# A hybrid decoder step on one core: state loads moved within the scans, and one activation table loaded ahead

## The chip, the cores and the metric

The kernel runs on one core of a Trainium2 chip. The metric is device time in microseconds (us), the median of several runs; less is better. The core's engines are called by these names in the profile: PE is TensorE (matmuls; PEld is its weight load), DVE is VectorE, ACT is ScalarE, POOL is GpSimd, SP is SyncE. Each works through a queue of its own in order. Here SyncE and GpSimd also issue nearly all the DMAs; "POOLq" and "SPq" are the issuing sides of these engines.

## The reference

One layer of a hybrid decoder for a prompt of 256 tokens and for 8 samples of 4 tokens each, which share the weights. Cut to what matters here:

```python
xn = _rmsnorm(x, norm_mix)
z, xbc, dt_raw, q, k, v, r, g_lr, gate_a, gate_b = _split(xn @ w_in, IN_SIZES)
xbc = silu(causal_dwconv(xbc));  xs, Bm, Cm = _split(xbc, ...)
dt = softplus(dt_raw + ssd_dt_bias);  A = -exp(ssd_A_log)
y_ssd, ssd_state_new = _ssd_scan(xs_h, dt, A, Bm, Cm, ssd_state)       # 4 groups of 8 heads
u = (y_ssd + ssd_D * xs_h) * silu(z)
u = u * rsqrt(mean(u * u, axis=-1) + EPS) * ssd_norm                   # per group
branch_a = u @ w_ssd_out
glog = log_sigmoid(g_lr @ w_gla_gate + b_gla_gate) / GATE_TAU
o, gla_state_new = _gla_scan(qh, kh, vh, glog, gla_state)              # 4 heads
o = o * rsqrt(mean(o * o, axis=-1) + EPS) * gla_norm * silu(r)
branch_b = o @ w_gla_out
h = x + (sigmoid(gate_a) * branch_a + sigmoid(gate_b) * branch_b) @ w_mix_out
h = h + cross_attend(_rmsnorm(h, norm_cross), mem_k, mem_v, w_cq, w_co)
up = causal_dwconv(_rmsnorm(h, norm_ffn) @ w_up);  a, gt = split(up)
h = h + (silu(gt) * a) @ w_down
```

All states (`state_ssd`, 8 samples x 32 heads x 64 x 128, and others) are read and their new values written.

## The kernel before

All activations are held transposed, channels on partitions and the 288 tokens (256 of the prompt, 32 of the samples) along the free axis. A projection (`proj`, lines 133 to 169) runs over blocks of 256 output columns and, inside, over the 16 blocks of input channels, two at a time: `wload` (108) has SyncE load 256 KB of weights into one of six `raw` buffers; `wsplit` (100) lets ScalarE round them to `whi` (line 103) and VectorE subtract to `wlo` (105), five buffers of each; then 12 matmuls (148, 149, 153) of 288 columns use them up. When a block is done, ScalarE or VectorE copies its accumulators out of PSUM, for instance into `vT` (1044) or added into `ma` (1034).

The middle of the kernel (lines 1353 to 1364) goes through eight units n: four groups of the state-space branch (`ssd_scan`, line 743) and four heads of the gated linear attention (`gla_scan`, 1109). While the scan of unit n runs in the background, step by step (`weave`, 176), the main stream projects the inputs of unit n+1 (`ssd_proj`, `gla_proj`), then after 16 steps the output of unit n-1 (`project`), and in some units a few blocks of the gate (`gate_early`, 1295, with a Tanh on ScalarE for each block t and a store to `ga_d`). In n=2 and n=3 the first 20 background steps have TensorE's order written out by hand; everything else is put in order by a planner, which simulates the engines and issues what is ready, earlier lines first. DMAs marked `keep_in_program_order` stay in the order of the program.

A state-space scan first loads decays (`load_decay`, 749, tile `ab`, and `mab`, 759), transposes B, C and x, forms the decay matrices `m` (856, 859: Relu and Exp on ScalarE) in a loop over u = 0, 1, 2, whose products run one u later (870 to 892), and after that loop turns to the samples. Their states come twice: as `sin` by `load_state` (762; 2 DMAs of 256 KB for two samples, updated at 951 and stored at 956 by SyncE), and as `sqr` by `load_square` (772; 4 DMAs of 64 KB for one sample, transposed by VectorE into `st` at 941 for the products of line 927). `sin` and `m` share the six buffers of tag `c4`; `ab`, `sqr`, the gates and others share the seven of `e2`. GpSimd issues all these loads.

Each scan ends in `finish` (1005): the sum of squares by a matmul with ones (1013), `rstd_from` (230: logarithm at 232, exponential at 233), then the scaling into `un` (1021, 197, 198), which the output projection reads. `decays` (1058) of a GLA head uses Exp and Ln (1070, 1071) and later Exp (1077). Before the FFN `rstd_of` (1473) forms one more such norm. An activation function needs its table in ScalarE; where the set that is loaded lacks the function, the build puts an ACT_TABLE_LOAD in front, under the line of the function. Line 286 loads the set `LNEXP` ahead, for the norms of the first part.

Of the kernel before, what the change touches and what calls it, by code (L numbers as in the profile page):

```python
# [8 lines left out]
F32 = mybir.dt.float32  # L9
# [7 lines left out]
P = 128  # L17
# [25 lines left out]
def hybrid_step(ctx: ExitStack, tc: tile.TileContext, I: dict, O: list):  # L43
# [31 lines left out]
    ones = const.tile([P, P], F32, name="ones")  # L75
    V.memset(ones, 1.0)
    epsc = const.tile([P, 3], F32, name="epsc")
    V.memset(epsc[:, 0:1], EPS)
    V.memset(epsc[:, 1:2], 4.0 * EPS)
    fold4 = const.tile([P, NS], F32, name="fold4")  # L80
# [145 lines left out]

    def two(u, n):
        return lambda k: (u[:, k, :], u[:, n + k, :])

    def rstd_from(pl, ssq, n, four=False):  # L230
        r = pl.tile([P, T], F32, tag="rstd", bufs=1, name="rstd")
# [453 lines left out]
    def rep4(src, name):  # L685

        n = src.shape[1]
        o = b2(name).rearrange("p (t r s) -> p t r s", r=4, s=NS)[:, 0:n]
        V.tensor_copy(o, src.unsqueeze(2).to_broadcast([P, n, 4, NS]))
        return o.rearrange("p t r s -> p t (r s)")  # L690
# [52 lines left out]
    def ssd_scan(g, xsT, sz):  # L743
# [18 lines left out]
        def load_state(q):  # L762
            sin = c4([P, 2, 512], "sin")
            for e in range(2):
                tc.keep_in_program_order(G.dma_start(
                    out=sin[:, e, :].rearrange("p (t n) -> p t n", n=P),
                    in_=I["state_ssd"][2 * q + e, h0:h0 + 8].rearrange("(t e) x n -> (e x) t n", e=2)))
            sins.append(sin)
# [11 lines left out]


        bsr = rep4(bT[:, SEQ:T].unsqueeze(1), "bsr")
        yield
        a = mm_tile()
        MM(a[:, 0:256], bT[:, 0:P], cT[:, 0:SEQ], start=True, stop=True)
# [61 lines left out]
        for u in range(3):  # L847
            if u < 2:
                m = c4([P, 4, SEQ], "m")
                ea = b2("ea").rearrange("p (r n) -> p r n", n=P)  # L850
                for w in range(2):
                    ab, rr = abs_[2 * u + w], slice(2 * w, 2 * w + 2)
                    for r in range(2):
                        h = h0 + 4 * u + 2 * w + r
                        for c in range(2):
                            S.activation(m[:, 2 * w + r, c * P:(c + 1) * P], ab[:, r, c * P:(c + 1) * P], ACT.Relu,
                                         scale=-1.0, bias=tokc[:, c, 32 + h:33 + h])
                    S.activation(ea[:, rr], ab[:, :, P:SEQ], ACT.Exp)
                    S.activation(m[:, rr], m[:, rr], ACT.Exp, scale=-1.0)
                    if u == 0:  # L860
                        load_decay(2 + w)
                    yield
                    V.tensor_tensor(m[:, rr], m[:, rr],
                                    cbm.rearrange("p c n -> p (c n)").unsqueeze(1).to_broadcast([P, 2, SEQ]), ALU.mult)
                    V.tensor_tensor(ea[:, rr], ea[:, rr], cbx.unsqueeze(1).to_broadcast([P, 2, P]), ALU.mult)
                    yield
            if prev is not None:
                uu, pm, pea = prev
                a = mm_tile()
                for w in range(2):  # L870
                    o = w * SEQ
                    for s in range(3):
                        for e in range(2):
                            q = 2 * w + e
                            hs = slice((4 * uu + q) * 64, (4 * uu + q + 1) * 64)
                            rows = slice(64 * e, 64 * e + 64)
                            if s == 0:
                                MM(a[rows, o:o + P], xdt[0][:, hs], pm[:, q, 0:P], start=True, stop=True)
                            elif s == 1:
                                MM(a[rows, o + P:o + SEQ], xdt[1][:, hs], pm[:, q, P:SEQ], start=True, stop=False)  # L880
                            else:
                                MM(a[rows, o + P:o + SEQ], wx[0][:, hs], pea[:, q, :], start=False, stop=True)
                if u == 2:
                    axs = mm_tile()
                    for t in range(4):
                        TR(axs[:, t * P:(t + 1) * P], xsr[:, t, :], ident)
                for w in range(2):
                    tt = 2 * uu + w
                    tmp = th_tile()
                    V.scalar_tensor_tensor(tmp[:, 0:SEQ], xsT[:, tt, 0:SEQ], dcol[:, 4 * g + tt:4 * g + tt + 1],  # L890
                                           a[:, w * SEQ:(w + 1) * SEQ], ALU.mult, ALU.add)
                    V.tensor_tensor(sz[:, tt, 0:SEQ], tmp[:, 0:SEQ], sz[:, tt, 0:SEQ], ALU.mult)
            if u < 2:
                prev = (u, m, ea)
            if u == 1:
                xsr = rep4(xsT[:, :, SEQ:T], "xsr")
            yield
        for b in range(NSQ):
            load_square(b)
        load_state(0)  # L900
        load_state(1)

        diag(cdm, cT[:, SEQ:T])
        for r in range(2):
            S.activation(mss[:, r, :], mab[:, r, :], ACT.Relu, scale=-1.0, bias=acs[:, 2 * g + r:2 * g + r + 1])
# [27 lines left out]
        for hf_ in range(2):  # L933
            bblk = r2("bblk").rearrange("p (b n) -> p b n", n=P)
            V.tensor_tensor(bblk, bst.unsqueeze(1).to_broadcast([P, 4, P]),
                            bmask[:, 4 * hf_:4 * hf_ + 4].unsqueeze(2).to_broadcast([P, 4, P]), ALU.mult)
            pair = sins[2 * hf_:2 * hf_ + 2]

            def turned(b):
                st = b2("st")  # L940
                V.transpose(st, sqs[b])
                if b + NSQ < NB:
                    load_square(b + NSQ)
                sts.append(st)

            def updated(t):
                a = mm_tile()
                MM(a, wst[:, t * P:(t + 1) * P], bblk.rearrange("p b n -> p (b n)"), start=True, stop=True)  # L948
                for b in range(4):
                    sl_ = pair[b // 2][:, b % 2, t * P:(t + 1) * P]  # L950
                    V.scalar_tensor_tensor(sl_, sl_, elcol[:, 4 * g + t, 4 * hf_ + b:4 * hf_ + b + 1],
                                           a[:, b * P:(b + 1) * P], ALU.mult, ALU.add)
                if t % 2:
                    for b in range(4):
                        hh = h0 + 2 * (t - 1)
                        nc.sync.dma_start(
                            out=o_sssd[4 * hf_ + b, hh:hh + 4].rearrange("(t e) x n -> (e x) t n", e=2),
                            in_=pair[b // 2][:, b % 2, (t - 1) * P:(t + 1) * P].rearrange("p (t n) -> p t n", n=P))

            for x in range(4):  # L960
                turned(4 * hf_ + x)
                yield 1.5
                if x % 2 == 0:
                    continue
                for t in ((0, 1) if x == 1 else (2, 3)):
                    updated(t)
                    if hf_ == 0 and t < 2:
                        load_state(2 + t)
                    yield 1.5
        inter()  # L970
        yield
# [33 lines left out]
    def finish(u, sq, gcol, four):  # L1005

        if len(fin) < 7:
            sp = b2r("sqh")[:, 0:T], b2r("sql")[:, 0:T]
            split(*sp, sq)
            yield  # L1010
            ssq = mm_tile()
            for w in range(2):
                MM(ssq[:, 0:T], ones.bitcast(F32R), sp[w], start=(w == 0), stop=(w == 1))
        else:
            ssq = mm_tile()
            MM(ssq[:, 0:T], ones, sq, start=True, stop=True)
        rstd = rstd_from(pa, ssq[:, 0:T], 512, four)
        yield
        un = pa.tile([P, 8, T], F32R, tag="un", bufs=1, name="un")
        for t in range(4):  # L1020
            V.tensor_tensor(u[:, t, :], u[:, t, :], rstd, ALU.mult)
            split_from(un[:, t, :], un[:, 4 + t, :], u[:, t, :], gcol[:, t:t + 1])
            if t % 2:
                yield
        fin.append(un)
# [14 lines left out]
    def gla_proj(h, out):  # L1040
# [17 lines left out]
        def decays():  # L1058
# [8 lines left out]
                S.activation(qe[:, k, :], a[:, 0:T], ACT.Identity, bias=vec("b_gla_gate")[:, 2 * h + k:2 * h + k + 1])  # L1067
            yield
            S.activation(ke, qe, ACT.Abs)
            S.activation(ke, ke, ACT.Exp, scale=-1.0)  # L1070
            S.activation(ke, ke, ACT.Ln, bias=1.0)
            V.scalar_tensor_tensor(qe, qe, 0.0, ke, ALU.min, ALU.subtract)
# [217 lines left out]
            yield from proj(I["w_in"], o + 256 * j2, 256, X, KT, cons)  # L1290

    gq = []
    GH = KT // 4

    def gate_early(t, a):

        if t % 2 == 0:
            gq.append(e2("gq"))
        S.activation(gq[-1][:, t % 2, :], a, ACT.Tanh, scale=0.5)
        if t % 2:  # L1300
            G.dma_start(out=ga_d[:, t - 1:t + 1, :], in_=gq[-1])

# [169 lines left out]

    def rstd_of():
        ssq = mm_tile()
        tc.keep_in_program_order(MM(ssq[:, 0:T], ones, rst.pop(), start=True, stop=True))
        return rstd_from(pb, ssq[:, 0:T], D)

    rst = []
# [508 lines left out]
```

## Time and profile before

| | us |
|---|---|
| median of 3 runs | 2479.48 (2479.35 to 2480.06) |
| the profiled execution | 2484.3 |
| its span | 2482.6 |
| TensorE busy in it | 2466.2 |
| ScalarE busy in it | 1355.8 |

The span is what the trace covers, from the first to the last instruction; the execution's own time is 1.7 us longer. The profiled execution is 4.8 us above the median of the runs without a profile. A matmul's end is modelled, so busy time of PE counts matmuls that overlap only once. In a row by line stand the line, the engine, the operation, its tiles (out<-in), how often, then busy us and mean ns, then the idle time before. In a row of waits stand who waited, for whom, the total, the times and the longest. In a row by stretch stand the stretch, the sum, each engine's busy time with its number of instructions, the granted clock of PE (1.00 is full), the mean busy share of the 16 DMA engines, and GB/s.

### The profile page before, as it was taken

The page shows a single profiled execution, that of the slowest core. Times are in us where ns is not written, and L with a number is a line of the kernel's source. Part 1 is how long each engine was busy: PE and PEld are TensorE (multiplying, and loading weights), DVE is VectorE, ACT ScalarE, POOL GpSimd, SP SyncE. Part 2 cuts the span into 40 slices and gives each one's busy share as a digit, 9 for nine tenths or more (in the row PEclk, how much of TensorE's full clock was granted, in tenths as well). Part 3 has the DMA queues.
Part 4 walks back from the last instruction along what each step waited for, and adds up shares of the span by engine and source line. Part 5 has one row for each costly group of instructions (what it writes and reads, how often), then busy time and mean ns, then how long its engine had stood idle before and what let it go on. Part 6 is the DMA issues. An engine that isn't in the chain of part 4 may idle for free.

```text
span 2482.6 us, 52113 instructions
## 1 busy us (share of the span) xinstructions
PE 2466.2 (99%) x18738; PEld 2388.1 (96%) x18738; DVE 1775.2 (72%) x3804; ACT 1355.8 (55%) x2781; POOL 439.2 (18%) x798
## 2 busy tenths in 40 slices
PE   9999999999999999999999999999999999999998
PEld 8889999999999999999999989999999999999998
DVE  6866778896777766777666577667777676676766
ACT  6766647646464655554455545455555454554545
POOL 3102144143111010110111122402111001020012
PEclk9999999999999999999999999999999999999999
DMA  8877697787768686777778599655555555555555
GB/s 261 263 234 208 165 267 217 208 246 223 223 211 287 207 255 194 240 246 229 224 230 266 182 353 327 196 164 171 170 171 172 171 171 173 170 172 168 170 173 170
DMA packets 457652, 530.77 MB, mean 214 GB/s; under 512 B 40316, under 2 KB 403676, under 8 KB 457360
## 3 DMA queue, kind: packets, MB, share of 16 engines
q1 hardware_dynamic: 420272, 422.39, 56.6%
q0 software_dynamic: 37088, 105.03, 13.2%
q8 instruction: 147, 2.41, 0.4%
q14 instruction: 113, 0.93, 0.1%
q10 hardware_dynamic: 32, 0.01, 0.0%
HBM read 476.41 MB, written 50.86 MB: 212 GB/s over the span
## 4 chain that ended last, share of the span: by engine, by line
PE 96%; DMA 1%; DVE 1%; issue 0%; ACT 0%; SPq 0%; POOL 0%; DVEq 0%; ACTq 0%; POOLq 0%
PE acc L149 28%; PE acc L148 27%; PE acc L153 27%; PE acc L348 2%; PE acc L352 2%; PE acc L349 2%; PE mm L1263 1%; PE la L1254 1%; PE la L1606 1%; DMA kc<-in_cache_mem_k_dram 1%; PE mm L1218 0%; DMA raw<-in_w_ssd_out_dram 0%; PE la L1664 0%; PE la L927 0%; PE mm L948 0%
## 5 line engine op out<-in xcount | busy, mean ns | idle before, releaser
L103 ACT CAST whi<-raw 128x512 fp32r<-128x512 f32 x1464 | 898.1, 618 | 951.5 <-PE acc L149 786.1
L105 DVE TENSOR_TENSOR wlo<-raw,whi 128x512 fp32r<-128x512 f32 x1464 | 995.4, 686 | 534.3 <-ACT whi L103 527.0
L149 PE MATMUL acc<-xn,whi 128*128 128x288 f32 (+1 forms) x1936 | 541.6, 295 | 0.0
L148 PE MATMUL acc<-xn,whi 128*128 128x288 f32 (+1 forms) x1936 | 540.1, 294 | 0.3 <-ACT whi L103 0.3
L153 PE MATMUL acc<-xn,wlo 128*128 128x288 f32 (+1 forms) x1936 | 409.0, 293 | 0.0
L149 PE MATMUL acc<-hf,whi 128*128 128x288 f32 x1408 | 393.3, 296 | 0.0
L148 PE MATMUL acc<-hf,whi 128*128 128x288 f32 x1408 | 388.6, 292 | 0.0
L148 PEld LDWEIGHTS acc<-xn,whi 128*128 128x128 f32 (+1 forms) x1936 | 363.4, 188 | 4.9 <-issue 3.1
L149 PEld LDWEIGHTS acc<-xn,whi 128*128 128x128 f32 (+1 forms) x1936 | 363.7, 188 | 3.6 <-issue 0.4
L153 PEld LDWEIGHTS acc<-xn,wlo 128*128 128x128 f32 (+1 forms) x1936 | 310.4, 188 | 0.8 <-issue 0.4
L153 PE MATMUL acc<-hf,wlo 128*128 128x288 f32 x1408 | 294.5, 290 | 0.0
L149 PEld LDWEIGHTS acc<-hf,whi 128*128 128x128 f32 x1408 | 264.5, 188 | 0.0
L148 PEld LDWEIGHTS acc<-hf,whi 128*128 128x128 f32 x1408 | 264.0, 188 | 0.0
L153 PEld LDWEIGHTS acc<-hf,wlo 128*128 128x128 f32 x1408 | 226.4, 188 | 0.1
L149 PE MATMUL acc<-pr,whi 128*128 128x288 f32 x704 | 196.6, 295 | 0.0
L148 PE MATMUL acc<-pr,whi 128*128 128x288 f32 x704 | 194.8, 293 | 0.0
L1780 POOL COPY fsp<-fst 128x16 f32<-128x16 f32 x88 | 38.5, 440 | 651.8 <-DVE av L1792 433.4
L153 PE MATMUL acc<-pr,wlo 128*128 128x288 f32 x704 | 147.3, 290 | 0.0
L148 PE MATMUL acc<-un,whi 128*128 128x288 f32 x512 | 143.7, 296 | 3.3 <-ACT vT L1044 2.4
L149 PE MATMUL acc<-un,whi 128*128 128x288 f32 x512 | 143.7, 296 | 0.0
L149 PEld LDWEIGHTS acc<-pr,whi 128*128 128x128 f32 x704 | 132.3, 188 | 0.0
L148 PEld LDWEIGHTS acc<-pr,whi 128*128 128x128 f32 x704 | 132.0, 188 | 0.0
(564 smaller groups left out, 4318.4 us busy)
## 6 DMA issues: line engine op xcount, KB each, us to landing
raw<-in_w_in_dram SPq DMA_DIRECT2D x480, 256.0 KB
raw<-in_w_up_dram SPq DMA_DIRECT2D x352, 256.0 KB
raw<-in_w_down_dram SPq DMA_DIRECT2D x176, 256.0 KB
raw<-in_w_ck_dram SPq DMA_DIRECT2D x64, 256.0 KB
raw<-in_w_cv_dram SPq DMA_DIRECT2D x64, 256.0 KB
raw<-in_w_ssd_out_dram SPq DMA_DIRECT2D x64, 256.0 KB
sin<-in_state_gla_dram POOLq DMA_DIRECT2D x32, 512.0 KB, 6.4
out_dram<-sin SPq DMA_DIRECT2D x32, 512.0 KB
```

The costliest lines, as they stand in the source:

```text
L103: S.copy(hi, raw)
L105: V.tensor_tensor(lo, raw, hi, ALU.subtract)
L148: MM(a, hi[:, k, cs], xh, start=(k0 + s0 + k == 0), stop=False)
L149: MM(a, hi[:, k, cs], xl, start=False, stop=False)
L153: MM(a, lo[:, k, cs], xh, start=False, stop=(k0 + s0 + k == nk - 1))
L348: MM(accs[m], mn_hi[:, kk, ms_], hi[:, 0, :], start=(kk == 0), stop=False)
L349: MM(accs[m], mn_lo[:, kk, ms_], hi[:, 0, :], start=False, stop=False)
L352: MM(accs[m], mn_hi[:, kk, ms_], lo[:, 0, :], start=False, stop=(kk == KT - 1))
L1254: MM(osa[NS * j:NS * j + NS, :], qdm[:, k, b, :], sins[b][:, k, :], start=False, stop=(q == 1 and k == 0))
L1263: MM(a, kb[:, k * P:(k + 1) * P], vst, start=True, stop=True)
L1606: MM(ssc[NS * c:NS * c + NS, 0:P], xq[:, j, u, :], kt[:, j], start=(j == 0), stop=(j == 15))
L1780: G.tensor_copy(sp[:, :, 0:2], st.rearrange("p (b k) -> p b k", k=2))
```

## The change

Three things are changed in the state-space scan. All four `load_state` calls stand at its beginning, behind the loads of the decays and before its first step. The two first `load_square` calls stand in the last part of u = 1 instead of behind the loop. The `load_state` calls behind the loop and in the update are gone.

A helper `lnexp` loads the set `LNEXP`, if wanted behind a copy of one column on ScalarE that depends on a given tile. It is called in `finish` for the first seven units behind the matmul of the sum of squares (in the first and third, after a wait in the step order until the main stream has formed another pair of gate tiles), in `decays` between Abs and Exp, and in `rstd_of` ahead of its matmul. `tanhs` counts the Tanhs of `gate_early`.

```diff
+    junk1 = const.tile([P, 1], F32, name="junk1")
...
+    def lnexp(after=None):
+
+        if after is not None:
+            S.copy(junk1, after)
+        tc.keep_in_program_order(S.preload_act_table_set(LNEXP))
...
         bsr = rep4(bT[:, SEQ:T].unsqueeze(1), "bsr")
+        for q in range(4):
+            load_state(q)
         yield
...
             if u == 1:
                 xsr = rep4(xsT[:, :, SEQ:T], "xsr")
-            yield
-        for b in range(NSQ):
-            load_square(b)
-        load_state(0)
-        load_state(1)
-
+                for b in range(NSQ):
+                    load_square(b)
+            yield
         diag(cdm, cT[:, SEQ:T])
...
                     updated(t)
-                    if hf_ == 0 and t < 2:
-                        load_state(2 + t)
                     yield 1.5
...
                 MM(ssq[:, 0:T], ones.bitcast(F32R), sp[w], start=(w == 0), stop=(w == 1))
+            if len(fin) in (0, 2):
+                after = len(gq)
+                while len(gq) == after or len(tanhs) % 2:
+                    yield
+                lnexp(gq[-1][:, 1, 0:1])
+            else:
+                lnexp(sp[1][:, 0:1])
         else:
...
             S.activation(ke, qe, ACT.Abs)
+            lnexp()
             S.activation(ke, ke, ACT.Exp, scale=-1.0)
...
+    tanhs = []
...
         S.activation(gq[-1][:, t % 2, :], a, ACT.Tanh, scale=0.5)
+        tanhs.append(t)
...
     def rstd_of():
         ssq = mm_tile()
-        tc.keep_in_program_order(MM(ssq[:, 0:T], ones, rst.pop(), start=True, stop=True))
+        a = rst.pop()
+        lnexp(a[:, 0:1])
+        tc.keep_in_program_order(MM(ssq[:, 0:T], ones, a, start=True, stop=True))
         return rstd_from(pb, ssq[:, 0:T], D)
```

## The prediction

> **What bounds the kernel now.** I read the page first, for the engines' shares.
>
> ```profile
> span 2482.6 us, 52113 instructions
> ...
> PE 2466.2 (99%) x18738; PEld 2388.1 (96%) x18738; DVE 1775.2 (72%) x3804; ACT 1355.8 (55%) x2781; POOL 439.2 (18%) x798
> ```
>
> TensorE is busy for 99% of the span. Neither edit adds or removes a matmul of the projections, so the time can fall only where TensorE stands still or runs slowly. ScalarE is idle for 45%: what a table load costs it matters only where somebody waits. The second view is what TensorE waited for, between 600 and 645 us:
>
> ```profile
> PE acc L148 <- ACT vT L1044: 2.4, 1, 2.4
> PE acc L148 <- DVE ma L1034: 1.0, 1, 1.0
> PE acc L148 <- ACT whi L103: 0.3, 1, 0.3
> ```
>
> Over the whole span no other wait of TensorE is as long as the first. These three fall in the fourth scan (group 3 of the state-space branch, n=3), which starts near 586 us. The third view, busy time by stretch (sum, then PE, PEld, DVE, ACT, POOL, clock, DMA share, GB/s), prices them:
>
> ```profile
> 600.00:605.00 5.00, 4.69 (x39) 4.46 (x38) 4.94 (x11) 5.00 (x14) 1.96 (x4) 1.00 0.75 222
> 620.00:625.00 5.00, 2.65 (x16) 2.42 (x16) 0.74 (x2) 1.54 (x3) 1.92 (x4) 0.89 0.96 234
> 625.00:630.00 5.00, 5.00 (x44) 4.66 (x43) 4.79 (x11) 1.86 (x3) 2.47 (x4) 0.77 0.88 257
> 630.00:640.00 10.00, 9.02 (x82) 8.49 (x81) 9.00 (x20) 3.00 (x5) 2.57 (x4) 1.00 0.48 142
> ```
>
> Idle TensorE: 5.00-4.69 = 0.31, 5.00-2.65 = 2.35, 10.00-9.02 = 0.98, together 3.64 us. After the long gap the granted clock falls: (1-0.89)x5 + (1-0.77)x5 = 0.55+1.15 = 1.70 us more. **5.3 us is all that these edits can return** (0.21% of the time). [...]
>
> Why TensorE stood still shows on ScalarE's timeline:
>
> ```profile
> 587.77 0.41 ACT L1299 ACTIVATE gq<-acc 128x288 f32<-128x288 f32 x1
> 588.82 0.62 ACT L103 CAST whi<-raw 128x512 fp32r<-128x512 f32 x1 [0.65 <-ACT gq L1299]
> 589.46 1.28 ACT L232 ACT_TABLE_LOAD   x1
> 590.75 0.50 ACT L232 ACTIVATE rstd<-mm,epsc 128x288 f32<-128x288 f32 x1
> 591.15 1.27 ACT L856 ACTIVATE m<-ab,tokc 128x128 f32<-128x128 f32 x4
> 592.45 1.28 ACT L233 ACT_TABLE_LOAD   x1
> 593.74 0.44 ACT L233 ACTIVATE rstd<-rstd 128x288 f32<-128x288 f32 x1
> ...
> 622.53 0.62 ACT L103 CAST whi<-raw 128x512 fp32r<-128x512 f32 x1 [3.21 <-DMA raw<-in_w_ssd_out_dram]
> 623.06 0.39 ACT L1044 COPY vT<-acc 128x288 f32<-128x288 f32 x1
> ```
>
> The copy vT that TensorE waited 2.4 us for stands behind a weight cast that itself waited 3.21 us for its weights. So the gap is a late DMA. It is late for two reasons. First, the loads of sample states share the DMA engines (POOL's timeline, then the stretch view, by which the engines' share is above 1):
>
> ```profile
> 596.37 2.99 POOL L765 DMA_DIRECT2D sin<-in_state_ssd_dram  x4
> ...
> 609.96 2.99 POOL L765 DMA_DIRECT2D sin<-in_state_ssd_dram  x4
> ```
>
> ```profile
> 613.00:623.00 10.00, 8.15 (x63) 7.92 (x61) 2.08 (x3) 2.63 (x5) 5.16 (x8) 1.00 1.06 306
> ```
>
> Second, SyncE issues a weight load only when one of six raw buffers is free, and the casts and subtractions that free them stood in a pile-up: ScalarE was full (5.00 of 5 in the first stretch above), and VectorE first idled for the norm and was then full (4.94). So SyncE issued 11 loads in 26.26 us, one in 2.39:
>
> ```profile
> 580.23 26.26 SPq L110 DMA_DIRECT2D raw<-in_w_in_dram  x11
> ```
>
> ```profile
> 594.22 1.56 DVE L1021 TENSOR_TENSOR sz<-sz,rstd 128x288 f32<-128x288 f32 x4 [4.05 <-ACT rstd L233]
> ```
>
> **The change, part by part.** *States first.* Four load_state calls, 8 DMAs of 256 KB (2.1 MB), leave the tail of each state-space scan for its head; POOL's issue cost is 2 x 2.99 = 6.0 us a scan as before. At 306 GB/s they fill all DMA engines for 6.9 us. Where do they go? Bufs=6 of c4 hold four states and two m tiles, so the loads of scan g+1 may go as soon as scan g's m tiles are read and its states stored. The planner does pull ready loads far ahead:
>
> ```profile
> L759 POOL DMA_DIRECT2D mab<-acum_d x16: 539/542/559, 199.0 to 465.0; - x16
> ```
>
> The last of the mab loads, for the scan that starts near 586, went out at 465. So I expect the fourth scan's states between 540 and 575, in the tail of the third scan. They meet that scan's stores there:
>
> ```profile
> 330.00:345.00 15.00, 15.00 (x116) 14.92 (x115) 10.79 (x22) 7.03 (x13) 1.55 (x3) 1.00 1.04 299
> 434.00:450.00 16.00, 16.00 (x122) 15.88 (x121) 12.49 (x29) 6.76 (x13) 1.35 (x5) 1.00 0.89 244
> 540.00:555.00 15.00, 15.00 (x112) 14.73 (x112) 14.43 (x39) 5.17 (x9) 6.68 (x11) 1.00 1.09 310
> 570.00:585.00 15.00, 15.00 (x118) 13.20 (x117) 10.06 (x21) 7.72 (x17) 2.60 (x4) 1.00 0.64 169
> ```
>
> The engines are nearly full or full there already, yet TensorE lost nothing. For the third scan the same 2.1 MB leaves the head of that busy stretch (its own states go earlier) and other 2.1 MB joins its end; 570 to 585 has 0.36 x 15 = 5.4 us of engine time free. I cost this at nothing; cover is the weights that are read ahead, up to six raw buffers. If the cover goes, the price is the gap seen at 620: 2.35+1.70 = 4.05 us for one scan. At 613 to 623 the moved traffic would take away 1 MB (the four at 610), 3.4 us at 306 GB/s, which is more than the 2.35 us gap: the gap goes.
>
> What queues behind a moved load: on POOL's in-order queue a state load that waits for its slot holds the ab loads and the copies of lines 664 to 670. The wait is bounded by the landing of a transfer of these tiles:
>
> ```profile
> DMA to landing us min/median/max: 3.4/5.7/8.3
> ```
>
> so 0 to 8.3 us on POOL, which is 82% idle; line 856 first reads ab at 591.15 in the fourth scan and the state loads go well before, so I take nothing. The m tiles now come after the states in the ring: ScalarE's L856 could wait for a store of the scan before, but SyncE issues nothing but weights from 580.23, so the last store left over 10.9 us before, and lands in 8.3 at most; nothing, by the same rows. *Squares one step earlier:* same DMAs, same order, no slot gained; nothing, between minus and plus 0.7 us (an issue of the larger kind, 2.99/4).
>
> *Tables.* The loads that the edit touches:
>
> ```profile
> L232 ACT ACT_TABLE_LOAD x9 | 11.5, 1283 | 0.2
> L233 ACT ACT_TABLE_LOAD x9 | 11.5, 1283 | 0.2
> ...
> L1071 ACT ACT_TABLE_LOAD x4 | 5.1, 1283 | 0.1
> L1077 ACT ACT_TABLE_LOAD x4 | 5.1, 1283 | 0.1
> ...
> L674 ACT ACT_TABLE_LOAD x1 | 1.3, 1283 | 0.0
> ```
>
> The combined set is loaded by line 286 and the first Tanh (L674) needed a load, so it has no Tanh. Each of seven norms, four decays and the last norm gets one load ahead in place of two inside, and gives one back at the next Tanh: 7 come back in the projections. Norm and decay of a GLA head share the set, so of 9+9+4+4 = 26 loads about 21 stay (2 at the unchanged eighth norm, 12 ahead, 7 given back), or 17 if those ahead into a loaded set are dropped: 5 to 9 x 1.283 = 6 to 12 us off ScalarE, which nobody waits for, except here: after the last gate Tanh (587.77+0.41 = 588.18) come a one-column copy (0.2, an estimate below that Tanh's 0.41 for 288 columns), the cast 0.62, the load 1.28, logarithm 0.50, exponential 0.44, 588.18+0.2+0.62+1.28+0.50+0.44 = 591.2 for rstd instead of 593.74+0.44 = 594.18. **Three microseconds** earlier for VectorE, which idled 4.05 us, and for the cast behind. The 0.31 us goes, and the weight loads after the pile-up are issued up to 3 us earlier: a second cover for the same gap. The copies into junk1 wait, in ScalarE's queue, for VectorE's sql or for a gate's Tanh: casts stand behind them, for 0 to 0.5 us each; the five buffers of whi hide it. The loop that holds the norm of scans 0 and 2 until the gate's pair is done delays un by the rest of its projection; un is read 16 steps into the next.
>
> [...]
>
> **Sum.** Returned: 0.31 + 2.35 + 1.70 = 4.36 us. The 0.98 us I leave: there VectorE ran four transposes ahead of the accumulation TensorE waited for, an order of the planner's:
>
> ```profile
> 634.76 2.48 DVE L941 STREAM_TRANSPOSE st<-sqr 128x512 f32<-128x512 f32 x4
> ```
>
> The profiled execution took 2484.3 us (span 2482.6 and 1.7 around it), so 2479.9 after it; the median without the profiler is 2479.48, 4.8 us less, and I take the same 4.36 off: **2475.1 us**. Whether the gap is as long without the profiler no view shows.
>
> **Rivals.**
> - *All of it.* With squares landing earlier the transposes are no longer bunched, and the 0.98 us goes too: 2479.48-5.34 = 2474.1. For it: transposes and weights shared those DMA engines. Against: the order is the planner's.
> - *The pile-up stays.* The gap is owed to ScalarE's and VectorE's burst, which is only shifted, or to the profiler's own traffic, or the planner leaves the state loads late; then 0 to 1.3 us (one load) returns: about 2479. For it: SyncE's 2.39 us a load, where TensorE takes one in 1.53 (below). [...]
> - *A new gap takes its place* in the third scan's tail (1.09 share and 2.1 MB more): 2475.1+4.05 = 2479.2.
> - *Slower.* The states meet stores and squares in the tails of three scans (the 1.04, 0.89 and 1.09 rows), and each weight load takes longer than what is read ahead: 3 x 4.05-4.36 = +7.8, 2487.3. It decides from the point where six raw buffers do not cover a landing; 12 matmuls use a buffer up, and 118 took 15.00 us from 570 to 585, so a buffer lasts 1.53 us and six last 9.2.
>
> **How the numbers follow.** Forecast 0.42, all of it 0.16, pile-up stays 0.20, new gap 0.12, slower 0.10. About 0.2% (5.0 us, to 2474.5) is what a measurement here tells from no change. The forecast lies 0.6 us short of that, so a quarter of it and all of the first rival count as faster: 0.11+0.16 = 0.27. Slower is 0.10, and the rest, 0.63, is within. The range goes from all of it less 0.7 us for the squares, 2473.4, to a new gap while of the old one the clock's 1.70 and the 0.31 stay lost, 2479.2+2.0 = 2481.2; the slower case is left out.
>
> **What would show it.** Right: no wait of TensorE over 0.5 us between 595 and 640, clock 1.00 throughout, state loads out before 586, rstd's exponential right behind its logarithm, one load by the next Tanh. Wrong: state loads still behind the squares; weight casts waiting for DMA near 550; TensorE gaps in the tails of the first three scans; a Tanh between a load ahead and its logarithm, which would bring two loads back.

## The result, and the profile after

The changed kernel takes **2488.12 us** (2486.35 to 2491.40, 7 runs) beside 2480.06 (2479.35 to 2483.04, 7 runs) for the kernel before: ratio 1.003, 95% interval 1.002 to 1.004, slower by 8 us. The forecast was 2475.1, with a range up to 2481.2. Of all executions reported below two were slow, one of `tables` (4958.83 us) and one of `after_merged` (6313.97): the ratios leave them out, the medians do not (without them 2498.0 and 2479.56).

The page of the profiled execution (2491.4 us) begins so:

```profile
span 2489.7 us, 52126 instructions
...
PE 2470.1 (99%) x18738; PEld 2389.4 (96%) x18738; DVE 1775.8 (71%) x3804; ACT 1353.0 (54%) x2788; POOL 442.2 (18%) x798
```

The work is the same (18738 matmuls). Idle TensorE grew from 2482.6-2466.2 = 16.4 us to 2489.7-2470.1 = 19.6, and its busy time, whose ends are modelled, by 3.9. A better measure is the distance from the start of a matmul to the start of the next, taken behind the matmuls of 128 by 128 weights with 288 or 512 columns: where it exceeds the usual 131 ns (227 for 512 columns) by over 40 ns, the excess adds up to 21.6 us before and 27.4 after, 5.8 of the 7.1 us by which the span grew. This sum is called the *gaps* below.

The pile-up that the forecast was about is gone. By stretch (sum, PE busy, clock, DMA share, GB/s), the changed kernel:

```profile
600.00:605.00 5.00, 5.00 (x43) 1.00 0.80 242
620.00:625.00 5.00, 5.00 (x40) 1.00 0.98 210
625.00:630.00 5.00, 5.00 (x40) 1.00 1.14 187
630.00:640.00 10.00, 10.00 (x102) 1.00 1.04 266
```

TensorE is full and at full clock in all four. But look at the last two columns: the DMA engines are at least as busy as before at 620 to 630 (0.96 and 0.88 then), and move less (234 and 257 then). That is the trail. New gaps stand elsewhere, as TensorE's waits from 310 to 660 us show:

```profile
PE mm L987 <- DVE ys L981: 2.7, 1, 2.7
PE acc L149 <- ACT whi L104: 2.3, 3, 1.0
PE acc L149 <- DVE ma L1045: 1.7, 2, 1.4
```

(Lines have moved: whi 103 is 104 now, load_state 765 is 772, load_square 777 is 784.) The first looks like VectorE; ScalarE's timeline just ahead of it, and the chain that ended last between 572 and 583 us, say otherwise:

```profile
574.45 0.62 ACT L104 CAST whi<-raw 128x512 fp32r<-128x512 f32 x1 [2.37 <-DMA raw<-in_w_in_dram]
...
576.07 0.62 ACT L104 CAST whi<-raw 128x512 fp32r<-128x512 f32 x1 [0.69 <-DMA raw<-in_w_in_dram]
578.22 1.29 ACT L104 CAST whi<-raw 128x512 fp32r<-128x512 f32 x2 [1.53 <-DMA raw<-in_w_in_dram]
```

```profile
569.42 8.70 DMA raw<-in_w_in_dram
...
578.89 0.63 ACT whi L104
...
579.55 0.69 DVE wlo L106
580.24 0.60 DVE ys L978
...
581.07 0.39 DVE ys L981
```

The casts wait for weights, VectorE's subtractions wait for the casts, and the scan's own `ys` stands behind them in VectorE's queue. Over the whole span ScalarE waited for these weights this long (total us, times, longest), before and after:

```profile
ACT whi L103 <- DMA raw<-in_w_in_dram: 21.0, 19, 2.9
```

```profile
ACT whi L104 <- DMA raw<-in_w_in_dram: 53.9, 33, 6.2
```

The weights come late, 33 times instead of 19. In the stretch from 540 to 555, where the forecast quoted 1.09 of share and 310 GB/s, the changed kernel has

```profile
540.00:555.00 15.00, 14.41 (x103) 1.00 1.10 245
```

about the same share and a fifth fewer bytes. The states did go where the forecast put them (GpSimd's timeline):

```profile
547.01 2.99 POOL L772 DMA_DIRECT2D sin<-in_state_ssd_dram  x4
559.73 2.98 POOL L772 DMA_DIRECT2D sin<-in_state_ssd_dram  x4 [9.73 <-DMA raw<-in_w_in_dram]
```

GpSimd stood still for 9.73 us ahead of the second half, more than the 8.3 us that the forecast had as its bound.

So the rival "slower" (2487.3) seemed to be right: states in the tails starve the weights. The experiments show that it was not.

### The profile page after: what moved, and what is told of

Read it like the earlier page. It is cut to its first block, busy times and chain, and to the rows that moved or that the text cites. A ratio compares the mean times of both kernels' runs of the same rounds, so it can differ in the third digit from the quotient of the medians.

```text
span 2489.7 us, 52126 instructions
## 1 busy us (share of the span) xinstructions
PE 2470.1 (99%) x18738; PEld 2389.4 (96%) x18738; DVE 1775.8 (71%) x3804; ACT 1353.0 (54%) x2788; POOL 442.2 (18%) x798
## 4 chain that ended last, share of the span: by engine, by line
PE 93%; DMA 4%; DVE 1%; ACT 1%; issue 1%; POOL 0%; DVEq 0%; SPq 0%; ACTq 0%; POOLq 0%
PE acc L150 27%; PE acc L149 26%; PE acc L154 26%; DMA raw<-in_w_in_dram 2%; PE acc L355 2%; PE acc L359 2%; PE acc L356 2%; DMA raw<-in_w_ck_dram 1%; PE la L1266 1%; PE la L1622 1%; PE la L1680 1%; PE mm L1275 1%; DVE wlo L106 1%; PE mm L1230 0%; DMA sin<-in_state_gla_dram 0%
```

## The experiments

Times are medians; each ratio is to the kernel before, run together with the kernels of the same group (medians 2481.44, 2480.85, 2481.77 and 2480.78 in the four groups).

**First group: which part costs it?** Three theories. A: state loads in the tails starve the weights. B: the squares, no longer broken up by state loads, do. C: the norms' tables and what follows them. `tables` is the logarithm and exponential part alone, `states` the moved loads alone; the other two hold each state load back until its scan has begun, by a one-element copy ahead of it, with and without the tables:

```diff
             sin = c4([P, 2, 512], "sin")
+            G.tensor_copy(sin[:, 0, 0:1], bsr[:, 0, 0:1])
             for e in range(2):
```

`tables`: 

> The table loads ahead alone; state and square loads stand where they stood before. Theory A (the state loads, pulled into the tail of the scan before, take the DMA engines from the weights): 2478 to 2481 us, the gap near 621 us of the kernel before is still there (2 to 3 us), no new gaps at 443 and 578. Theory B (the squares, no longer broken up by state loads, do it): the same. Theory C (the norms behind a wait and the loads ahead put ScalarE and VectorE into a worse order): 2484 us or more.

`states`: 

> The moved state and square loads alone; no table is loaded ahead. Theories A and B: 2485 to 2490 us, as the whole change (2488.1), with ScalarE waiting over 10 us for weights between 410 and 460 us (7.3 us in the kernel before) and TensorE gaps there. Theory C: 2482 us or less.

`held`: 

> The whole change, but each state load is tied to its scan's start by a GpSimd copy of one column from bsr into its tile. The squares stay unbroken. Theory A: the loads leave the tails, 2475 to 2480 us, no gap at 443 us. Theory B: 2484 to 2490 us, the gap at 443 us stays, since 32 square loads still follow each other there.

`states_held`: 

> As held, without the table loads ahead. Theory A: 2476 to 2481 us; theory B: 2484 to 2490 us. The difference to held prices the tables: within 2 us by A and B, over 3 us slower or faster by C.

| kernel | us | ratio, 95% |
|---|---|---|
| tables | 2498.9 | 1.0068 (1.0054 to 1.0081) |
| states | 2480.58 | 0.9997 (0.9989 to 1.0006) |
| held | 2488.06 | 1.0027 (1.0016 to 1.0038) |
| states_held | 2482.21 | 1.0001 (0.9992 to 1.0010) |

A and B fell: the states and squares alone cost nothing, and holding the states back regains nothing (`held` lies in B's range, but `states` and `states_held` exclude B). The loss belongs to the half that touches no DMA, as C has it. And yet `tables` shows slow DMAs. Its waits of TensorE, and the stretch from 540:

```profile
PE acc L149 <- ACT whi L104: 7.3, 5, 5.0
PE acc L149 <- DVE ma L1048: 2.7, 1, 2.7
...
PE acc L355 <- ACT whi L104: 1.0, 1, 1.0
```

```profile
540.00:555.00 15.00, 14.05 (x105) 1.00 1.11 251
```

GpSimd's instructions in `tables` stand in the same order as before. The wait of line 355 ends at 75 us, in the projections of the memory; the first instruction of an edited line runs at 377 us. So the cause acts before the edited code runs: it must be something static. The built programs differ in one such thing: `junk1`, one float a partition, takes 32 bytes right behind `epsc`, and **every tile allocated later lies 32 bytes higher**. `after`, `held` and `tables` have it; `states` and `states_held` do not. (The earlier state loads also move the buffers of `sin` and `m`, from 0 to 128 past a multiple of 256 bytes; `states` has that and loses nothing.)

**Second group: theory D, the addresses.** `shift32` and `shift64` are the kernel before with such a tile and nothing else; `packed` and `tables_packed` are the change and its table half with the scratch column inside `epsc`, whose 12 bytes leave room in their 32:

```diff
-    epsc = const.tile([P, 3], F32, name="epsc")
-    junk1 = const.tile([P, 1], F32, name="junk1")
+    epsc = const.tile([P, 4], F32, name="epsc")
+    junk1 = epsc[:, 3:4]
```

```diff
+    junk1 = const.tile([P, 1], F32, name="junk1")     # shift64: [P, 16]
     V.memset(epsc[:, 0:1], EPS)
+    V.memset(junk1, 0.0)
```

`shift32`: 

> The kernel before with one tile more: a scratch tile of four bytes a partition, behind the column of constants, written once by VectorE at the start and read by nobody. No table is loaded elsewhere, no state and no square is moved. In the built programs it puts every tile that comes after it 32 bytes higher in SBUF, as the change and its table half do, so that the staging tiles of the weights no longer start on a multiple of 64 bytes. D (the address: DMA writes that start 32 bytes off are slower, and the weights arrive late): 2488 to 2500 us, near the 2498.9 of the table half, with a gap of TensorE behind the cast to whi, and in 540 to 555 us about 250 GB/s at a DMA share of 1.1, not the 310 of before. C (the tables' place and the copies on ScalarE cost it): 2479 to 2482 us, as before.

`shift64`: 

> As shift32, but the tile has 64 bytes a partition, and everything after it lies 64 bytes higher. D, if it is the multiple of 64 that counts: 2479 to 2483 us, as before. D, if a larger multiple counts (128 or more, since the weights' staging tiles started on a multiple of 256): 2485 us or more. C: 2479 to 2482 us, so shift32 must tell C from the first form of D.

`tables_packed`: 

> The table half alone, with its scratch element put into a fourth column of the constants' tile (which fills up its 32 bytes), so that every tile lies where it lay before. All twelve table loads and their copies stay. D: 2474 to 2481 us, without the 5.0 us gap at 564 us that the table half has. C: 2495 us or more, as the table half's 2498.9.

`packed`: 

> The whole change with the same fourth column: tables, states and squares as in the change, addresses as before. D: 2474 to 2481 us, that is the forecast of the change as it stood, and no gap of TensorE behind the weights' casts in 540 to 580 us. C: 2486 to 2491 us, as the change.

| kernel | us | ratio, 95% |
|---|---|---|
| shift32 | 2504.26 | 1.0098 (1.0083 to 1.0114) |
| shift64 | 2503.09 | 1.0092 (1.0078 to 1.0106) |
| tables_packed | 2481.06 | 1.0003 (0.9994 to 1.0012) |
| packed | 2479.43 | 0.9995 (0.9987 to 1.0004) |

D holds from both sides, and C falls: the addresses alone cost the old kernel 23 us, and without them neither the tables nor the whole change costs anything. A multiple of 64 bytes is not enough: `shift64` has 1.0092.

At the shifted addresses, though, the edits are not neutral. The kernel before stands at 1.0098 there, the table half (`tables`) at 1.0068 and the whole change at 1.003: by these ratios, taken in different groups, the table half takes off some 7 us of the loss and the states' half 9 more. Why was not tested.

**Third group: which multiple, which tiles?** `shift128` as above with `[P, 32]`. `weights32` moves only `raw`, `whi` and `wlo` (and six small constants ahead of them) by 32 and all later tiles by 128 (32 bytes ahead, 96 behind); `rest32` moves only what comes behind them, by 32.

`shift128`: 

> The kernel before with a scratch tile of 128 bytes a partition behind the constants' column, written once at the start; everything after it lies 128 bytes higher (the weights' staging tiles at 384 past a multiple of 512, before 256). D128 (what counts is a start on a multiple of 128 bytes): 2479 to 2483 us, as before. D256 (a multiple of 256 counts for the weights): 2490 us or more. E (any tile more at this place costs it, wherever it moves the others): 2498 to 2506 us, as the shifts by 32 and 64.

`weights32`: 

> The kernel before with 32 bytes more ahead of the weights' staging and split tiles and 96 bytes more behind them: only raw, whi and wlo are 32 bytes off, every later tile (activations, states, squares, caches) lies exactly 128 bytes higher than before. Dw (the weights' transfers are what gets slow): 2495 to 2505 us. Dr (the others): 2479 to 2484 us. If both carry part of it, in between, and the two losses of weights32 and rest32 add up to about 23 us.

`rest32`: 

> The kernel before with 32 bytes more behind the weights' tiles: raw, whi and wlo lie where they lay, and every later tile is 32 bytes higher. Dw: 2479 to 2484 us. Dr (the other transfers get slow, the states', caches' and masks' on the gpsimd queue, and hold up the weights behind them): 2495 to 2505 us.

| kernel | us | ratio, 95% | gaps, us |
|---|---|---|---|
| shift128 | 2487.53 | 1.0023 (1.0015 to 1.0032) | 24.2 |
| weights32 | 2529.2 | 1.0190 (1.0176 to 1.0204) | 26.8 |
| rest32 | 2535.28 | 1.0216 (1.0202 to 1.0230) | 29.6 |

No theory had this: `shift128` lies between two expected ranges, and `weights32` and `rest32` lose more than moving all tiles by 32 cost. The gaps do not hold the loss of these two: 5.2 and 8.0 us more than the 21.6 of before. The rest is in the matmuls themselves. From 1750 to 2400, where nothing waits, the kernel before, `weights32` and `rest32` have

```profile
1750.00:2400.00 650.00, 650.00 (x5002) 1.00 0.58 171
```

```profile
1750.00:2400.00 650.00, 650.00 (x4878) 1.00 0.56 166
```

```profile
1750.00:2400.00 650.00, 650.00 (x4877) 1.00 0.56 166
```

At the same clock 650 us hold 5002 or 4878 matmuls: 129.9 ns each or 133.3. What `weights32` and `rest32` share is that weights and activations no longer lie alike: `whi` at 288 past a multiple of 512 bytes and `xn` at 384, or 256 and 288. In every other kernel `whi` and `xn` lie alike (both at 256 before, both at 288 in the change), and the late part of the change and of `shift128` runs at the old pace (5002 matmuls each). What differs is the place within 128 bytes: successive blocks of `xn` lie 1152 bytes apart, so in every kernel they take four places, 128 bytes apart. This is a second effect, which the change does not have. It spoils the times of these two runs as a test of the weights' transfers; the rates of their DMAs, below, suffer less.

**Fourth group: the squares.** Their rows are 128 bytes long, the shortest of the states' loads. In `after_sq` only they go back onto a multiple of 128; in `before_sq32` only they leave it; `before_ab32` does that to the decays, whose rows are 1 KB. `after_merged` keeps the change whole and takes 32 bytes away behind `junk1`, by giving two other constants one tile:

```diff
-    dtb = const.tile([32, 1], F32, name="dtb")
-    alog = const.tile([32, 1], F32, name="alog")
+    dtal = const.tile([32, 2], F32, name="dtal")
+    dtb, alog = dtal[:, 0:1], dtal[:, 1:2]
```

```diff
-            sq_ = e2("sqr").rearrange("p a t -> p (a t)")[:, 0:512]
+            sq_ = e2("sqr").rearrange("p a t -> p (a t)")[:, 24:536]     # before_sq32: 8:520
```

`after_merged`: 

> The whole change with its scratch tile as it stands, and two other small constants, dtb and alog, put into one tile, so that one tile of 32 bytes goes away behind it and everything from the weights' staging tiles on lies where it lay before. D (only the addresses count): 2478 to 2482 us. E (a tile and a write more count, wherever the others lie): 2486 to 2491 us, as the change.

`after_sq`: 

> The whole change, with the squares of the states written 96 bytes further into their tiles, so that they start on a multiple of 128 bytes again; all else stays 32 bytes high. Dsq (the squares, whose rows are 128 bytes long, carry the loss): 2479 to 2483 us. Dother (the decays, states and weights carry it): 2486 to 2491 us. If both do, in between.

`before_sq32`: 

> The kernel before with the squares written 32 bytes further into their tiles; no tile is added and every other address stays. Dsq: 2490 to 2506 us, with fewer GB/s than 310 in 540 to 555 us. Dother: 2479 to 2483 us.

`before_ab32`: 

> The kernel before with the broadcast decays (ab) written 32 bytes further into their tiles, every other address as before. Dsq: 2479 to 2483 us. Dother, as far as it is the decays: 2486 us or more.

| kernel | us | ratio, 95% |
|---|---|---|
| after_merged | 2479.6 | 0.9995 (0.9986 to 1.0004) |
| after_sq | 2483.73 | 1.0013 (1.0004 to 1.0022) |
| before_sq32 | 2488.11 | 1.0029 (1.0020 to 1.0038) |
| before_ab32 | 2481.03 | 1.0001 (0.9992 to 1.0009) |

E (an added tile costs something by itself) falls with `after_merged`: the change as written, 32 bytes back, takes 8.5 us less. The squares carry part of it: 7.3 us in the old kernel (2 us less than the least that was expected if they carried all), and 4 to 5 of the change's 8 (its ratio falls from 1.003 to 1.0013). VectorE's transposes, which read the moved squares, take as long as before (22.0 us in the change, which has them at 160 as well, against 22.1). The DMA view shows it (count, size, median us from issue to landing), for before and `before_sq32`,

```profile
sqr<-in_state_ssd_dram POOLq DMA_DIRECT2D x128, 64.0 KB, 5.1
```

```profile
sqr<-in_state_ssd_dram POOLq DMA_DIRECT2D x128, 64.0 KB, 6.3
```

and for the change, `after_sq` and `after_merged`:

```profile
sqr<-in_state_ssd_dram POOLq DMA_DIRECT2D x128, 64.0 KB, 5.7
```

```profile
sqr<-in_state_ssd_dram POOLq DMA_DIRECT2D x128, 64.0 KB, 3.9
```

```profile
sqr<-in_state_ssd_dram POOLq DMA_DIRECT2D x128, 64.0 KB, 3.8
```

The wait of ScalarE for weights follows: 53.9 us in the change, and in `after_sq` and `after_merged`

```profile
ACT whi L104 <- DMA raw<-in_w_in_dram: 32.9, 20, 5.2
```

```profile
ACT whi L104 <- DMA raw<-in_w_in_dram: 26.5, 18, 6.3
```

To compare all the kernels, here is what the DMA engines moved while they were full: the mean GB/s of all stretches of 10 us (18 to 33 of them in a kernel) in which the packets' time, summed over 16 engines, makes a share above 1.0. Starts are given past a multiple of 256 bytes.

| kernel | raw starts at | squares start at | GB/s when full |
|---|---|---|---|
| before; before_ab32; tables_packed | 0 | 128 | 342; 342; 342 |
| packed; after_merged; states; states_held | 0 | 128 | 341; 336; 339; 348 |
| after_sq | 32 | 0 | 321 |
| shift128 | 128 | 0 | 317 |
| weights32 | 32 | 0 | 317 |
| before_sq32 | 0 | 160 | 316 |
| rest32 | 0 | 160 | 304 |
| shift32; after; tables; held | 32 | 160 | 295; 296; 299; 302 |
| shift64 | 64 | 192 | 299 |

Each is compared with the kernel in place that has the same order of loads. Squares moved by 32 with all else in place: 26 GB/s less. Squares on a multiple of 128 with the weights off a multiple of 256: 15 to 25 less. Both: 40 to 47, close to the sum. The decays, whose rows are 1 KB and which load half as many bytes as the squares (16 times 256 KB, not 128 times 64 KB), keep the 342 when moved by 32. Why a start off these multiples lowers the rate, and why the squares' start counts and the decays' does not, was not shown.

What stays open: the weights' share was not isolated, since all three kernels with the squares in place and `raw` off 256 move other tiles as well; and `rest32`, 12 GB/s below `before_sq32`, may say that some other transfer pays too, but the kernels in place differ by as much (336 and 348).

## Why the prediction was wrong

**The step that failed is the cost of the table half's scratch column.** It was costed as "a one-column copy (0.2, ...)" and copies into `junk1` of "0 to 0.5 us each; the five buffers of whi hide it". As an instruction that is right: `tables_packed` keeps every copy and load and takes 2481.06, ratio 1.0003. As a tile it moved all later ones by 32 bytes, and the same loads then took longer on engines that were already full (a share of 1.10 from 540 to 555; the squares landed 5.7 us after their issue in the median, and after 3.8 in `after_merged`): with the 32 bytes taken back (`after_merged`) the change takes 8.5 us less. No term, and no rival, had the tile's place in memory. The forecast read the edit as instructions and queues only.

**States and squares at nothing: right.** They went into the tails at 547 and 559, as foreseen, and `states` is at 0.9997. The rival "slower" gave 2487.3 and the time came to 2488.1, by another cause: its mechanism is in `states`, which lost nothing at the old addresses. The size alone would have confirmed a wrong story.

**The 4.36 us returned: wrong, even with the addresses in place.** `packed` and `after_merged` are 1.4 and 1.2 us below before, and both intervals include no change. The old gap is gone in their profiles; but it was no steady part of the old kernel's time either. `before_ab32` issues the kernel before's instructions in the same order at the same rate (342 GB/s), and its profiled execution has, in the place where the forecast's row showed 2.65 of 5.00 busy,

```profile
620.00:625.00 5.00, 5.00 (x50) 1.00 1.11 273
...
630.00:640.00 10.00, 7.69 (x58) 1.00 0.37 108
```

and a span of 2478.0 where before's had 2482.6. TensorE does stand still there, 2.3 us near 636 us for `ma`, but no clock is lost: idle time from 600 to 640 is 2.62 us instead of 3.64, and the 1.70 us of clock are not paid. (It is one execution, and its decays lie 32 bytes off.) The forecast noted that the profiled execution lay 4.8 us above the median and that no view shows whether the gap is as long without the profiler, and then took the whole 4.36 off the median. Much of the 4.8 was probably the gap itself; that was not measured. The rival "the pile-up stays" (2479) comes nearest to the packed versions, though not by its mechanism.

**The 0.98 us left standing: right in kind.** In `after_merged` the wait for `ma` is still there, 2.3 us in two pieces:

```profile
PE acc L149 <- DVE ma L1045: 2.3, 2, 1.4
```

**Tables: partly wrong, and it did not matter.** In the norm that the forecast priced, a load still stands between logarithm and exponential, and the load "ahead" runs behind the norm (ScalarE's timeline of the change):

```profile
592.46 1.28 ACT L239 ACT_TABLE_LOAD   x1
593.75 0.50 ACT L239 ACTIVATE rstd<-mm,epsc 128x288 f32<-128x288 f32 x1
594.27 1.28 ACT L240 ACT_TABLE_LOAD   x1
595.56 0.44 ACT L240 ACTIVATE rstd<-rstd 128x288 f32<-128x288 f32 x1
...
600.53 0.19 ACT L234 COPY junk<-gq 128x1 f32<-128x1 f32 x1
600.74 1.28 ACT L235 ACT_TABLE_LOAD   x1
```

Its copy depends on a gate tile (line 1312) that this norm did not wait for: the step order held the norm back in the program, but the planner issued it first. The norm at 368.6 has the same. So the 3 us were not there: the exponential at 595.56 ended at 596.00, and before at 594.18. The copy itself took 0.19 us, as estimated. In all there are 31 loads where before had 32, not 5 to 9 fewer; ScalarE's busy time fell from 1355.8 to 1353.0, and nobody waited for the difference.

Neither `packed` nor `after_merged` beats the kernel before by more than the runs can tell.

## What to carry to other kernels

A new tile can also be a shift of every tile behind it (here by 32 bytes, which cost the old kernel 23 us): after an edit compare addresses, and put scratch into the padding of a tile that is there. When a kernel slows down in a place that the edit cannot reach, or moves fewer GB/s at the same DMA share (here 245 instead of 310, at 1.10 and 1.09), look at alignment before schedules; a change should be judged by its parts at equal addresses. And a gap of a few us seen in one profiled execution is worth its size only if the median carries it: compare the execution with the runs first.

## What the runs showed of the hardware

- **The rate of full DMA engines fell with the address that the squares were written to.** Moving the destination of these 128-byte rows by 32 bytes took it from 342 to 316 GB/s, moving that of the decays' 1 KB rows left it at 342; with all tiles moved it was 295.
- **TensorE's pace fell where weights and activations no longer lay alike.** With `whi` and `wlo` at 288 and the activations at 384 past a multiple of 512 bytes (or 256 and 288), a 128x288 matmul came every 133.3 ns instead of 129.9, at clock 1.00: over the kernel some 42 and 45 us, an estimate from the medians' loss of 47.4 and 53.5 less the gaps' 5.2 and 8.0, and more than any gap in it. By the distances between starts the matmuls with `wlo` carry most of it: those on `hf` came every 136.2 and 134.6 ns instead of 128.0, with `whi` every 131.9 and 132.7 instead of 131.0. Which tiles must lie alike was not isolated, and no other distances within 128 bytes were tried.
- **A gap did not always cost clock, and its length alone did not decide.** Before, around 2.35 us of idle from 620 to 625 the clock was 0.89, and 0.77 in the 5 us behind. In `tables_packed` the clock was 0.87 around a gap of 1.9 us (630 to 640). In the change, the 2.7 us ahead of line 987 cost none:

```profile
575.00:580.00 5.00, 3.79 (x29) 1.00 1.06 343
580.00:585.00 5.00, 3.49 (x26) 1.00 0.70 197
585.00:590.00 5.00, 5.00 (x41) 1.00 0.57 160
```
